# Expert part of a hybrid layer: the first slots' copies, a bank and row numbers in another order, and the second largest slot last, with the other second norms under its products

## Chip, cores and metric

The kernel runs on one core of one Trainium2 chip. The metric is the device time of one execution, in microseconds (us), as the median over runs.

## What is computed

One decoder layer over 1,024 rows of 1,024 numbers: attention over a sliding window beside a gated spatial mix, a first norm that gives h, then 32 experts of which each row uses four, and a second norm. Cut to the part that matters here:

```python
h = layer_norm(ALPHA * x + mix, ln1_g, ln1_b)
top_vals, top_idx = top_k(h @ w_router + b_router, 4)      # of 32 experts
gates = softmax(top_vals)
def expert(xb, e):                                         # rows xb of h sent to expert e
    gt = minimum(xb @ w_gate[e] + b_gate[e], 7.0)
    up = clip(xb @ w_up[e] + b_up[e], -7.0, 7.0)
    return (gt * sigmoid(1.702 * gt) * (up + 1.0)) @ w_down[e] + b_down[e]
y = layer_norm(ALPHA * h + sum of gates * expert rows, ln2_g, ln2_b)
```

## The kernel before, in words

The first 390 us or so hold projections, attention, first norm and router; the expert part fills the rest. The experts are sorted by their number of rows into 32 slots with fixed numbers of columns (`CAP`, 256 down to 88); a flag at the end tells whether one had too many, and `rescue` would then do its rows once more. `ORDER` says which slot is worked when: the largest and the smallest first, then pairs of a large and a small one, at the end the two of `LAST`.

A slot has three products: g and u (from the rows, to the hidden values) and d (back). Each is cut into two halves, so there are 192 pieces, in the order that `plan` writes out. A piece needs 2 MB of weights, loaded by SP's queue as two tiles into a ring of seven `raw` buffers (`loads`). ACT makes the upper half-precision part of each (`hi`, L962), DVE the rest (`lo`, L966), into one of three `wsp` buffers, two pieces ahead of PE. `multiply` (L1126) is 96 matmuls: four blocks of 128 outputs, eight steps, three products of parts. Its results lie in PSUM banks pg, pu or pd, two of each. ACT adds the bias to g (`gate1`, `gv`, L1158) and takes its gelu (`gate2`), DVE does u (`glu1`, `glu3`, `glu5`), the result is `hid`; DVE copies d to `yt` (`down`, L1199). PE turns `yt` (`turn`, L1209), ACT weights the rows (`combine`) and POOL scatters them, adding, into a tensor acc in memory, which started with ALPHA h.

A slot's rows are found and brought so: DVE writes a one-hot (`onehot`, L1081), PE multiplies it with the row numbers (`rows_of`, L1091), ACT writes indices and gates (`index`), POOL gathers (`gather`), PE transposes (`xpose`, L1112), ACT copies to `xt` (`xcopy`, L1117; in slot 0 DVE does one of each two). A list of events, `ev`, hangs these steps on the pieces; the tables in `SEQ` order the steps on one piece. All engines work strictly through their own rows in the order in which the program writes them. `rank` gives the places of the rows; its last part casts V on ACT and PP on DVE.

At the end the eight blocks of acc are loaded back (`loads`, L1006), two to a load, and normed: the `s` steps in `FIN` are sums on ACT and a power on POOL (`sums`, L1338 to L1342), the `a` steps two operations on DVE and a store (`first_norm`, L1351, L1352). Rows of the last slot aren't final in acc then: they are gathered apart to `xl`, get the slot's contribution (`last1`), sums (`last2`), their norm (`last3`, L1243, L1244) and are scattered over the output. DVE and PE write the flag (`flags`).

## Time and profile before

| | |
|---|---|
| median of 3 runs | 1703.27 us (1702.88 to 1704.67) |
| the profiled execution | 1707.27 us, span 1705.5 us |
| granted TensorE clock, mean | 0.974 of full speed |
| busy: PE, DVE, ACT, POOL | 1609.5 (94%), 1445.6 (85%), 1219.4 (72%), 310.2 us (18%) |
| DMA | 501.11 MB, mean 294 GB/s |

Times in the trace count from the start of the span. An engine is busy while it works on an instruction; waiting is not busy. A share is a mean over parts with different limits, so it tells which engine to look at and not what a change in one part is worth.

### The profile page before, as it was taken

To read this page: it belongs to the slowest core of one execution; us is meant where nothing else is said; L and a number is where in the kernel's file an instruction comes from. 1 tells how busy PE (TensorE), PEld (TensorE's weight loads), DVE (VectorE), ACT (ScalarE), POOL (GpSimd) and SP (SyncE) were. 2 spreads that over 40 slices of the span, in tenths; PEclk is the share of its full clock that TensorE was granted. 3 is DMA by queue.
4 is the path that set the end of the run, shared out by engine and by line. 5 is a ranking of instruction groups with operands and counts; after the bars stand their busy time and mean duration, and the time that the engine had idled before them with its cause. 6 is when DMAs were issued, how large, how long until landed. Compare 5 with 4: busy or idle time off the path is not lost.

```text
span 1705.5 us, 51018 instructions
## 1 busy us (share of the span) xinstructions
PE 1609.5 (94%) x21947; PEld 1509.6 (89%) x21947; DVE 1445.6 (85%) x2106; ACT 1219.4 (72%) x1662; POOL 310.2 (18%) x260
## 2 busy tenths in 40 slices
...
GB/s 270 91 122 38 164 99 100 87 322 197 226 348 338 329 324 337 343 343 343 339 355 338 364 343 373 364 361 371 358 364 352 377 339 382 361 382 359 366 348 139
DMA packets 86714, 501.11 MB, mean 294 GB/s; under 512 B 14210, under 2 KB 14226, under 8 KB 37330
## 3 DMA queue, kind: packets, MB, share of 16 engines
...
## 4 chain that ended last, share of the span: by engine, by line
PE 71%; ACT 3%; issue 1%; DVE 1%; DMA 1%; POOL 0%; POOLq 0%; DVEq 0%; ACTq 0%
PE pu L1126 22%; PE pg L1126 22%; PE pd L1126 21%; PE pt L1209 2%; PE pt L1112 2%; ACT wsp L962 1%; PE pt L1091 1%; DMA wsp<-htab,ix 1%; ACT xg L1338 0%; ACT gv L1158 0%; DMA raw<-w_d 0%; ACT xg L1340 0%; ACT y L1215 0%; DVE raw L1352 0%; ACT xt L1117 0%
## 5 line engine op out<-in xcount | busy, mean ns | idle before, releaser
L1126 PEld LDWEIGHTS <-wsp 128*128 128x128 f16 x18432 | 1152.7, 98 | 24.0 <-issue 9.6
L966 DVE SCALAR_TENSOR_TENSOR wsp<-raw,wsp 128x2048 f16<-128x2048 f32 x384 | 868.6, 2287 | 108.3 <-ACT wsp L962 102.4
L962 ACT ACTIVATE wsp<-raw 128x2048 f16<-128x2048 f32 x384 | 717.0, 1910 | 22.2 <-PE pu L1126 19.4
L1126 PE MATMUL pg<-xt,wsp 128*128 128x96 f16 (+30 forms) x6144 | 399.1, 226 | 4.2 <-ACT gv L1158 2.6
L1126 PE MATMUL pd<-hid,wsp 128*128 128x96 f16 (+30 forms) x6144 | 397.2, 226 | 4.2 <-ACT hid L1186 2.8
L1126 PE MATMUL pu<-xt,wsp 128*128 128x96 f16 (+30 forms) x6144 | 398.2, 226 | 0.0
L1217 POOL DMA_INDIRECT acc<-y,ix x49 | 99.7, 2034 | 820.7 <-ACT y L1215 534.2
L956 POOL DMA_INDIRECT xg<-htab,ix x49 | 78.7, 1607 | 257.4 <-ACT ixf L940 224.3
L1158 ACT ACTIVATE gv<-pg,bi 128x96 f32<-128x96 f32 (+30 forms) x256 | 78.7, 377 | 51.4 <-PE pg L1126 51.4
L1215 ACT ACTIVATE y<-pt,gw 128x512 f32<-128x512 f32 (+7 forms) x98 | 61.9, 685 | 41.9 <-PE pt L1209 41.9
L1117 ACT COPY xt<-pt 128x1024 f16<-128x1024 f16 (+29 forms) x98 | 70.8, 776 | 17.3 <-PE pt L1112 16.5
L1186 ACT ACTIVATE hid<-uv 128x384 f16<-128x384 f32 (+28 forms) x102 | 47.7, 499 | 43.6 <-DVE uv L1183 43.6
L179 DVE TENSOR_TENSOR wl<-rw,wh 128x512 fp32r<-128x512 f32 x56 | 38.8, 739 | 40.2 <-ACT wh L178 40.2
L198 PE MATMUL psp<-xh,wh 128*128 128x512 f32 x160 | 65.5, 409 | 6.8 <-ACT xh L189 6.8
L199 PE MATMUL psp<-xl,wh 128*128 128x512 f32 x160 | 65.2, 408 | 3.9 <-DVE xl L191 3.8
L948 ACT ACTIVATE ixf<-pt,dummy 128x1 f32<-128x1 f32 (+7 forms) x47 | 11.8, 251 | 75.9 <-PE pt L1091 75.9
L200 PE MATMUL psp<-xh,wl 128*128 128x512 f32 x160 | 64.5, 403 | 0.0
L1160 DVE SCALAR_TENSOR_TENSOR uv<-pu,bi 128x384 f32<-128x384 f32 (+28 forms) x102 | 53.7, 527 | 5.5 <-PE pu L1126 5.4
L527 PE MATMUL psp<-woh,mh 128*128 128x512 f32 x128 | 54.7, 428 | 3.5 <-issue 3.5
L1209 PE MATMUL pt<-iden,yt 128*128 128x128 f32 (+7 forms) x400 | 52.1, 273 | 2.6 <-ACT gv L1158 1.4
L1172 ACT ACTIVATE gv<-gv 128x384 f32<-128x384 f32 (+28 forms) x102 | 47.8, 512 | 8.2 <-DVE gv L1169 8.2
L529 PE MATMUL psp<-wol,mh 128*128 128x512 f32 x128 | 51.4, 402 | 1.1 <-DVE wol L489 1.1
...
## 6 DMA issues: line engine op xcount, KB each, us to landing
raw<-w_g SPq DMA_DIRECT2D x128, 1024.0 KB
raw<-w_u SPq DMA_DIRECT2D x128, 1024.0 KB
raw<-w_d SPq DMA_DIRECT2D x128, 1024.0 KB
...
```

The source lines that it names most:

```text
L198: nc.tensor.matmul(pt, wh[:, k], xh[h, k], start=(k == 0), stop=False)
L199: nc.tensor.matmul(pt, wh[:, k], xl[h, k], start=False, stop=False)
L200: nc.tensor.matmul(pt, wl[:, k], xh[h, k], start=False, stop=(k == 7))
L956: self.nc.gpsimd.indirect_dma_start(out=x[:m], out_offset=None, in_=self.htab, in_offset=bass.IndirectOffsetOnAxis(ap=self.IDX[j, o][:m], ...
L962: self.nc.scalar.activation(self.W[i][:, 0, 4 * z:4 * z + 4], self.RAW[i, z], AF.Copy, scale=WS)
L966: self.nc.vector.scalar_tensor_tensor(t[:, 1], self.RAW.pop((i, z)), WS, t[:, 0], op0=OP.mult, op1=OP.subtract, accum_out=self.FL[:, self. ...
L1117: (nc.vector.tensor_copy if j == 0 and z else nc.scalar.copy)(XT[j][:, z, :, o:o + m], XP.pop((j, o, z))[:, :, :m])
L1126: nc.tensor.matmul(out, w[:, wz, k, 128 * fc:128 * fc + 128], x[:, xz, k], start=(n == 0), stop=(n == 23))
L1158: nc.scalar.activation(out[:, q], src[:, q], AF.Identity, scale=1.0 / (HS * WS), bias=bi[:, c + q:c + q + 1])
L1209: nc.tensor.transpose(pt[:m, i], YT[j][:, 4 * g + i, o:o + m], self.iden)
L1215: nc.scalar.activation(y[:m, 512 * g:512 * g + 512], YP.pop((j, o, g))[:m].rearrange("p a b -> p (a b)"), AF.Copy, scale=GW[j, o][:m])
L1217: nc.gpsimd.indirect_dma_start(out=self.acc, out_offset=bass.IndirectOffsetOnAxis(ap=IDX[j, o][:m], axis=0), in_=y[:m], in_offset=None, co ...
```

## The change

Three things. **The first slots:** slot 1's transposes and copies go from ahead of the first product into its middle; the copy of slot 0's second 128 rows goes ahead of `rank`'s casts; g of slot 1 writes to a bank pd; the row numbers of slot 3 follow u of slot 0, and the indices of slots 2 and 3 come later in ACT's order; the gelu's table is loaded by a small extra activation. **The order of slots:** `LAST` ends with slot 244 columns wide instead of 124; the 124 goes into the pairs. **The end:** slot 30's d pieces come ahead of slot 31, whose six pieces stand last without a gap; `FIN` spreads the second norms over them; the last piece is cut into 128 and 116 columns, each turned, added and normed by itself with statistics from DVE. The scatter of the last slot's rows to acc is left to `rescue`. The diff, with pools, the rescue and removed functions cut:

```diff
@@ -29,8 +29,7 @@
 LA = 2
-FIN = {-3: ["s0", "s1"], -2: ["s2"], -1: ["s3", "a0", "a1"], 0: ["a2"],
-       1: ["c1", "s4", "s5", "a3", "s6", "a4", "c2", "s7", "a5", "a6", "a7", "c3"]}
+FIN = {-4: ["s0", "s1", "a0"], -3: ["s2", "s3"], -2: ["a1", "a2", "s4", "a3", "s5", "a4", "s6", "a5", "s7"]}
...
@@ -39,7 +38,7 @@
 ORD = ["q0", "q1", "k", "g0", "q2", "g1", "q3", "v", "u0", "u1", "u2", "u3"]
-LAST = [18, 19]
+LAST = [18, 1]
...
@@ -981,9 +980,9 @@
         s, e = NE - 2, NE - 1
-        seq += [("g", s, 0), ("d", s - 2, 0), ("u", s, 0), ("d", s - 2, 1), ("g", s, 1), ("d", s - 1, 0), ("u", s, 1),
-                ("d", s - 1, 1), ("g", e, 0), ("d", s, 0), ("d", s, 1), ("u", e, 0), ("g", e, 1), ("u", e, 1), None,
-                ("d", e, 0), ("d", e, 1)]
+        seq += [("g", s, 0), ("d", s - 2, 0), ("u", s, 0), ("d", s - 2, 1), ("g", s, 1), ("u", s, 1)]
+        seq += [("d", j, hf) for j in (s - 1, s) for hf in range(2)]
+        seq += [("g", e, 0), ("u", e, 0), ("g", e, 1), ("u", e, 1), ("d", e, 0), ("d", e, 1)]
...
@@ -1100,11 +1099,11 @@
 
-        XP = {}
+        XP, TL = {}, NE - 1
 
         def xpose(j, o, m):
             if o == 0:
-                XT[j] = pm.tile([128, 2, 8, CAP[j]], F16, name=f"xt{j % 2}", bufs=1)
+                XT[j] = pm.tile([128, 2, 8, CAP[j]], F16, name=f"xt{j % 2 if j < TL else 0}", bufs=1)
...
@@ -1139,11 +1138,18 @@
             for f, nf in groups(j):
-                pt = ps.tile([128, 512], F32, name="p" + kind, bufs=2)
+                pt = ps.tile([128, 512], F32, name="pd" if (kind, j, hf) == ("g", 1, 0) else "p" + kind, bufs=2)
                 pt = PG[kind, j, hf, f] = pt[:, :nf * n].rearrange("p (f n) -> p f n", n=n)
                 if (kind, j, hf) != ("d", NE - 1, 0):
                     for q in range(nf):
                         mm(pt[:, q], w, x, f + q)
+                if i == 0 and f == 0:
+                    for q, (o, m) in enumerate(subs(1)):
+                        xpose(1, o, m)
+                        xcopy(1, o, m)
+                if (kind, j, hf, f) == ("g", TL, 0, 0):
+                    turn(TL - 1, *subs(TL - 1)[0])
+                    combine(TL - 1, *subs(TL - 1)[0])
...
@@ -1210,40 +1216,71 @@
             m = whole(m)
-            y = pm.tile([128, D], F32, name="y", bufs=2)
+            y = pmm.tile([128, D], F32, name="y", bufs=2)
             for g in range(2):
                 nc.scalar.activation(y[:m, 512 * g:512 * g + 512], YP.pop((j, o, g))[:m].rearrange("p a b -> p (a b)"),
                                      AF.Copy, scale=GW[j, o][:m])
             nc.gpsimd.indirect_dma_start(out=self.acc, out_offset=bass.IndirectOffsetOnAxis(ap=IDX[j, o][:m], axis=0),
                                          in_=y[:m], in_offset=None, compute_op=OP.add)
 
-        TL = NE - 1
-
-        def last1(j):
-
-            m = whole(CAP[j])
-            y = self.yl = pm.tile([128, D], F32, name="y", bufs=2)
+        def last_turn(q, g):
+
+            o, m = subs(TL)[q]
+            pt = YP[q, g] = ps.tile([128, 4, 128], F32, name="pt", bufs=2)
+            for i in range(4):
+                nc.tensor.transpose(pt[:whole(m), i], YT[TL][:, 4 * g + i, o:o + whole(m)], self.iden)
+
+        def last_add(q, g):
+
+            cs = slice(512 * g, 512 * g + 512)
+            o, m = subs(TL)[q]
+            m = whole(m)
+            if g == 0:
+                self.yl.append((pmm.tile([128, D], F32, name="y", bufs=2), IDX[TL, o], m))
+            y, x = self.yl[q][0], self.xl[q]
+            nc.scalar.activation(y[:m, cs], YP.pop((q, g))[:m].rearrange("p a b -> p (a b)"), AF.Copy, scale=GW[TL, o][:m])
+            nc.vector.tensor_add(x[:m, cs], x[:m, cs], y[:m, cs])
+            nc.vector.bn_stats(self.lbn[:m, q, g], x[:m, cs])
+            if g:
+                self.scale1(self.lbn[:, q], self.lmv[:, q])
+
+        def last_norm(q):
+
+            x, mv, (y, ix, m) = self.xl[q], self.lmv[:, q], self.yl[q]
             for g in range(2):
                 cs = slice(512 * g, 512 * g + 512)
-                nc.scalar.activation(y[:m, cs], YP.pop((j, 0, g))[:m].rearrange("p a b -> p (a b)"),
-                                     AF.Copy, scale=GW[j, 0][:m])
-                nc.vector.tensor_add(self.xl[:m, cs], self.xl[:m, cs], y[:m, cs])
-
...
+                nc.vector.scalar_tensor_tensor(x[:m, cs], x[:m, cs], mv[:m, 0:1], self.l2g[:m, cs], op0=OP.subtract, op1=OP.mult)
                 nc.vector.scalar_tensor_tensor(x[:m, cs], x[:m, cs], mv[:m, 2:3], self.l2b[:m, cs], op0=OP.mult, op1=OP.add)
-            nc.gpsimd.indirect_dma_start(out=a["out"], out_offset=bass.IndirectOffsetOnAxis(ap=IDX[j, 0][:m], axis=0),
+            nc.gpsimd.indirect_dma_start(out=a["out"], out_offset=bass.IndirectOffsetOnAxis(ap=ix[:m], axis=0),
                                          in_=x[:m], in_offset=None)
+
+        def last_out(q, src):
+            o, m = subs(TL)[q]
+            nc.vector.scalar_tensor_tensor(YT[TL][:, 4:8, o:o + m], src, 1.0 / (ZS * WS), bc(BI[TL], 20, 4, m),
+                                           op0=OP.mult, op1=OP.add)
+
+        def last_piece():
+
+            w, pt = W.pop(n - 1), []
+            for q, (o, m) in enumerate(subs(TL)):
+                t = ps.tile([128, 512], F32, name="pg", bufs=2)
+                pt.append(t[:, :4 * m].rearrange("p (f n) -> p f n", n=m))
+                for f in range(4):
+                    mm(pt[q][:, f], w, HID[TL][:, :, :, o:o + m], f)
+                    if q and f == 1:
+                        last_turn(0, 1)
+                        last_add(0, 1)
+                if q == 0:
+                    for r in range(2):
+                        last_turn(r, 0)
+                    last_out(0, pt[0])
+                    for r in range(2):
+                        last_add(r, 0)
+            last_out(1, pt[1])
+            last_turn(1, 1)
+            last_norm(0)
+            last_add(1, 1)
+            last_norm(1)
...
@@ -1251,15 +1288,12 @@
             for k, (f, d) in enumerate(((onehot, 11), (rows_of, 10), (index, 9), (gather, 8)) if j > 1 else ()):
-                i = j - 2 + k // 2 if j < 4 else max(t - d, t0 + k)
-                ev.setdefault((i, f.__name__), []).append((f, (j,)))
+                i = (0, 0, 1, 1, 1, 2, 3, 3)[4 * j - 8 + k] if j < 4 else max(t - d, t0 + k)
+                ev.setdefault((i, "gather" if j < 4 and k == 2 else f.__name__), []).append((f, (j,)))
             for q, (o, m) in enumerate(subs(j)):
-                for f in (xpose, xcopy):
-                    ev.setdefault((max(t - 3 + q + (j == 2), q - 2 if j == 0 else 0), f.__name__), []).append((f, (j, o, m)))
-                if j == TL:
-                    ev.setdefault((at["d", j, 1] + 2, "turn"), []).append((turn, (j, o, m)))
-                    continue
-                for f in (turn, combine):
+                for f in (xpose, xcopy) if j != 1 else ():
+                    ev.setdefault((max(t - 3 + q + (j in (2, TL)), q - 2 if j == 0 else 0), f.__name__), []).append((f, (j, o, m)))
+                for f in (turn, combine) if j < TL - 1 else ():
...
@@ -1269,12 +1303,13 @@
         next(rank)
-        for i in range(-4, n + 4):
+        for i in range(-4, n):
             run(i, "index", "turn", "xpose")
             if i == -4:
                 next(rank)
             if i == -1:
                 lo(1, 0)
+                run(i, "xcopy")
...
@@ -1311,26 +1346,37 @@
                     run(i, st)
+            if i == n - 1:
+                self.flags1(pmm)
+                for b in (6, 7):
+                    self.first_norm("a", b)
+                last_piece()
+                break
+            if i == 0:
+                warm = pm.tile([128, 1], F32, name="warm")
+                nc.scalar.activation(warm, self.mhalf[:, 0:1], AF.Gelu_apprx_sigmoid)
             if 0 <= i < n and pieces[i][0]:
                 multiply(i)
             run(i, "rows_of")
             if i == n - 7:
                 self.norm_rows(*(x.bitcast(F32) for x in self.XT[:2]))
-                self.fmv = pmm.tile([128, 4, NB + 1], F32, name="fmv")
-                self.xl, self.junk = (x.bitcast(F32) for x in self.XT[2:])
-            if i == n - 5:
+                self.fmv = pmm.tile([128, 4, NB], F32, name="fmv")
+                self.lmv = pmm.tile([128, 2, 4], F32, name="lmv")
+                self.lbn = pmm.tile([128, 2, 2, 6], F32, name="lbn")
+                nc.vector.memset(self.lbn, 0.0)
+                self.xl, self.yl = [x.bitcast(F32) for x in self.XT[2:]], []
+                self.junk = pm.tile([128, D], F32, name="oh", bufs=1)
+            if i == n - 6:
                 self.summed = True
-                m = whole(CAP[TL])
-                nc.gpsimd.indirect_dma_start(out=self.xl[:m], out_offset=None, in_=self.acc,
-                                             in_offset=bass.IndirectOffsetOnAxis(ap=IDX[TL, 0][:m], axis=0))
+                for x, (o, m) in zip(self.xl, subs(TL)):
+                    m = whole(m)
+                    nc.gpsimd.indirect_dma_start(out=x[:m], out_offset=None, in_=self.acc,
+                                                 in_offset=bass.IndirectOffsetOnAxis(ap=IDX[TL, o][:m], axis=0))
             self.loads()
             for k in FIN.get(i - n, ()):
-                if k[0] == "c":
-                    (last1, last2, last3)[int(k[1]) - 1](TL)
-                else:
-                    self.first_norm(k[0], int(k[1]))
-        self.flags(pmm)
-        assert not ev
+                self.first_norm(k[0], int(k[1]))
+        self.flags2(pmm)
+        assert not ev, ev
...
@@ -1360,8 +1406,12 @@
         nc.vector.tensor_reduce(bs, bad, axis=AX.X, op=OP.max)
-        pt = self.psm.tile([128, 512], F32, name="pt", bufs=2)
-        nc.tensor.matmul(pt[:, 0:1], self.ones16, bs, start=True, stop=True)
+        self.bs = bs
+
+    def flags2(self, pm):
+        nc = self.nc
+        pt = self.psm.tile([128, 512], F32, name="pu", bufs=2)
+        nc.tensor.matmul(pt[:, 0:1], self.ones16, self.bs, start=True, stop=True)
```

The first place is ACT's order ahead of the first product and behind it: `raw` and `wsp` are the weights, `pt` is slot 0's and slot 1's transposed rows, `pd` `rank`'s places. Before:

```order
L962 ACTIVATE wsp_3274<-raw_3154 128x2048
L1117 COPY xt_3508<-pt 128x8x128
L1062 CAST V<-pd 128x4x32 x4
L1117 COPY xt_3508<-pt 128x8x128
L1117 COPY xt_3578<-pt 128x704 x2
L962 ACTIVATE wsp_3275<-raw_3271 128x2048
L962 ACTIVATE wsp_3275<-raw_3272 128x2048
L948 ACTIVATE ixf<-pt,dummy 128x1
```

and in the changed kernel:

```order
L961 ACTIVATE wsp_3274<-raw_3154 128x2048
L1116 COPY xt_3508<-pt 128x8x128 x2
L1061 CAST V<-pd 128x4x32 x4
L961 ACTIVATE wsp_3275<-raw_3271 128x2048
L961 ACTIVATE wsp_3275<-raw_3272 128x2048
L1357 ACT_TABLE_LOAD
L1357 ACTIVATE warm<-mhalf 128x1
L1116 COPY xt_3635<-pt 128x704 x2
L1164 ACTIVATE gv<-pg,bi 128x256 x4
```

The second copy of slot 0 (128x8x128) now stands ahead of the casts of V, and slot 1's two copies (128x704) behind both `hi` of the next piece and a row that loads a table.

The second place is DVE's order in the last slot (`xg_3276`, `xg_3277` hold the norm's scale and shift, `raw` a block of acc, `xg_3486`, `xg_3487` the last slot's rows). Before, around the last copies of `yt`, and from the last slot's norm on:

```order
L1199 SCALAR_TENSOR_TENSOR yt<-pd,bi 128x2x124 x2
L1351 SCALAR_TENSOR_TENSOR raw_3151<-raw_3151,fmv,xg_3276 128x1024
L1352 SCALAR_TENSOR_TENSOR raw_3151<-raw_3151,fmv,xg_3277 128x1024
L1230 TENSOR_TENSOR xg_3486<-xg_3486,y 128x512 x2
L1351 SCALAR_TENSOR_TENSOR raw_3151<-raw_3151,fmv,xg_3276 128x1024
...
L1243 SCALAR_TENSOR_TENSOR xg_3486<-xg_3486,fmv,xg_3276 128x512
L1244 SCALAR_TENSOR_TENSOR xg_3486<-xg_3486,fmv,xg_3277 128x512
L1243 SCALAR_TENSOR_TENSOR xg_3486<-xg_3486,fmv,xg_3276 128x512
L1244 SCALAR_TENSOR_TENSOR xg_3486<-xg_3486,fmv,xg_3277 128x512
L1359 TENSOR_SCALAR oh<-FL 128x384
L1360 TENSOR_SCALAR oh<-FH 128x8
```

In the changed kernel, from the copies of the first d piece on, and from the copy of the last 116 columns on:

```order
L1398 SCALAR_TENSOR_TENSOR raw_3152<-raw_3152,fmv,xg_3277 128x1024
L1205 SCALAR_TENSOR_TENSOR yt<-pd,bi 128x2x244 x2
L1405 TENSOR_SCALAR oh<-FL 128x384
...
L1398 SCALAR_TENSOR_TENSOR raw_3153<-raw_3153,fmv,xg_3277 128x1024
L1259 SCALAR_TENSOR_TENSOR yt<-pg,bi 128x4x128
L1242 TENSOR_TENSOR xg_3486<-xg_3486,y 128x512
L1243 BN_STATS lbn<-xg_3486 128x6
L1242 TENSOR_TENSOR xg_3487<-xg_3487,y 128x512
L1243 BN_STATS lbn<-xg_3487 128x6
```

```order
L1259 SCALAR_TENSOR_TENSOR yt<-pg,bi 128x4x116
L1252 SCALAR_TENSOR_TENSOR xg_3486<-xg_3486,lmv,xg_3276 128x512
L1253 SCALAR_TENSOR_TENSOR xg_3486<-xg_3486,lmv,xg_3277 128x512
...
L1242 TENSOR_TENSOR xg_3487<-xg_3487,y 128x512
L1243 BN_STATS lbn<-xg_3487 128x6
L1598 BN_AGGR lmv<-lbn 128x2
L1599 TENSOR_SCALAR lmv<-lmv 128x1
L1252 SCALAR_TENSOR_TENSOR xg_3487<-xg_3487,lmv,xg_3276 128x512
L1253 SCALAR_TENSOR_TENSOR xg_3487<-xg_3487,lmv,xg_3277 128x512
```

All the plain norms (L1397, L1398) now stand ahead of the last slot's final copies of `yt`, the flag rows too, and behind the last copy are the norms of the last slot's two parts alone.

## Rows read from the trace of the kernel before

**Rows 1.** Page: busy time of PE, and the chain that ended last, by line.

```profile
PE 1609.5 (94%) x21947; PEld 1509.6 (89%) x21947; DVE 1445.6 (85%) x2106; ACT 1219.4 (72%) x1662; POOL 310.2 (18%) x260
PE pu L1126 22%; PE pg L1126 22%; PE pd L1126 21%; PE pt L1209 2%; PE pt L1112 2%; ACT wsp L962 1%; PE pt L1091 1%; DMA wsp<-htab,ix 1%; ACT xg L1338 0%; ACT gv L1158 0%; DMA raw<-w_d 0%; ACT xg L1340 0%; ACT y L1215 0%; DVE raw L1352 0%; A
```

**Rows 2.** Busy us (rows) of PE, PEld, DVE, ACT, POOL; clock, DMA, GB/s; by stretch.

```profile
1500.00:1600.00 100.00, 98.57 (x1607) 98.12 (x1605) 95.06 (x114) 78.66 (x84) 12.40 (x9) 1.00 1.00 371
...
sum 1150.00, PE 1144.66 PEld 1133.95 DVE 1048.58 ACT 932.26 POOL 172.55; mean PE 95.39 PEld 94.50 DVE 87.38 ACT 77.69 POOL 14.38
```

**Rows 3.** Timeline of PE at the start: start, duration, instruction, wait before it.

```profile
390.64 0.74 PE L1112 MATMUL pt<-iden,xg 88*128 88x88 f16 x8 [1.76 <-ACT xt L1117]
392.22 0.75 PE L1112 MATMUL pt<-iden,xg 88*128 88x88 f16 x8 [0.83 <-ACT xt L1117]
392.80 12.73 PE L1126 MATMUL pg<-xt,wsp 128*128 128x256 f16 x96
...
408.61 3.92 PE L1126 MATMUL pg<-xt,wsp 128*128 128x88 f16 x96 [2.62 <-ACT gv L1158]
418.99 0.65 PE L1091 MATMUL pt<-V,oh 128*128 128x4 f16 x16 [6.46 <-DVE oh L1081]
419.57 16.76 PE L1126 MATMUL pu<-xt,wsp 128*128 128x256 f16 x192
...
436.93 3.33 PE L1126 MATMUL pg<-xt,wsp 128*128 128x256 f16 x29
```

**Rows 4.** Busy time at the start, columns as in rows 2.

```profile
396.00:397.00 1.00, 1.00 (x6) 0.71 (x5) 1.00 (x1) 1.00 (x1) 0.00 (x0) 0.50 0.00 0
397.00:398.00 1.00, 1.00 (x11) 0.88 (x9) 1.00 (x3) 0.35 (x1) 0.00 (x0) 0.95 0.00 0
424.00:425.00 1.00, 1.00 (x10) 0.81 (x8) 0.80 (x1) 1.00 (x3) 0.00 (x0) 0.79 0.41 156
```

**Rows 5.** Timeline of PE in the last slot.

```profile
1656.72 0.26 PE L1126 MATMUL pd<-hid,wsp 128*128 128x124 f16 x1 [2.82 <-ACT hid L1186]
...
1663.72 5.39 PE L1126 MATMUL pd<-hid,wsp 128*128 128x124 f16 x96 [1.19 <-DVE yt L1199]
```

**Rows 6.** Busy time in the last slot, columns as in rows 2.

```profile
1657.00:1660.00 3.00, 2.83 (x28) 2.83 (x28) 1.61 (x3) 3.00 (x2) 0.00 (x0) 0.50 1.03 419
```

**Rows 7.** Timeline of POOL at the end.

```profile
1643.28 1.91 POOL L1217 DMA_INDIRECT acc<-y,ix  x1 [13.17 <-ACT y L1215]
1651.28 1.80 POOL L1324 DMA_INDIRECT xg<-acc,ix  x1 [6.10 <-DMA acc<-y,ix]
...
1677.96 1.56 POOL L1342 TENSOR_TENSOR fmv<-fmv,mhalf 128x1 f32<-128x1 f32 x1
...
1684.42 0.55 POOL L1342 TENSOR_TENSOR fmv<-fmv,mhalf 128x1 f32<-128x1 f32 x1
...
1694.16 1.05 POOL L1245 DMA_INDIRECT out<-xg,ix  x1 [6.40 <-DVE flag L1372]
```

**Rows 8.** Timeline of DVE at the end.

```profile
1676.46 1.27 DVE L1351 SCALAR_TENSOR_TENSOR raw<-raw,fmv,xg 128x1024 f32<-128x1024 f32 x1
...
1679.03 1.28 DVE L1351 SCALAR_TENSOR_TENSOR raw<-raw,fmv,xg 128x1024 f32<-128x1024 f32 x1
...
1687.80 1.28 DVE L1352 SCALAR_TENSOR_TENSOR raw<-raw,fmv,xg 128x1024 f32<-128x1024 f32 x1 [0.81 <-POOL fmv L1342]
1689.00 0.74 DVE L1243 SCALAR_TENSOR_TENSOR xg<-xg,fmv,xg 128x512 f32<-128x512 f32 x1
```

**Rows 9.** Timeline of ACT at the start.

```profile
388.83 0.88 ACT L1062 CAST V<-pd 128x128 f16<-128x128 f32 x4 [4.05 <-DVE PP L1060]
389.56 1.03 ACT L1117 COPY xt<-pt 128x1024 f16<-128x1024 f16 x1
```

**Rows 10.** Timeline of PE: one product of a 244-column slot.

```profile
547.90 10.19 PE L1126 MATMUL pg<-xt,wsp 128*128 128x244 f16 x96
```

**Rows 11.** Waits of SP's queue, 437 to 1650: us in total, times, longest.

```profile
SPq L1018 <- DVE wsp L966: 869.8, 297, 8.6
```

More of the change, by code (lines that the diff above doesn't have):

```diff
@@ L838, in open_more @@
     def open_more(self):
-        p = self.pr2 = self.held.enter_context(self.tc.tile_pool(name="pr2", bufs=1, side="right"))
+        p = self.pr2 = self.held2.enter_context(self.tc.tile_pool(name="pr2", bufs=1, side="right"))
         self.RW += [p.tile([128, 4, 512], F32, name=f"raw{i}") for i in range(4, 7)]
@@ L1176, in glu1 @@
             if c == 0:
-                HID[j] = pm.tile([128, 2, 8, n], F16, name=f"hid{j % 2}", bufs=2)
+                HID[j] = pm.tile([128, 2, 8, n], F16, name=f"hid{j % 2 if j < TL else 0}", bufs=2)
             uv = UV[j, c] = tmp("uv", n, nf)
@@ L1226, in last1 @@
+        def last_norm(q):
+            x, mv, (y, ix, m) = self.xl[q], self.lmv[:, q], self.yl[q]
             for g in range(2):
                 cs = slice(512 * g, 512 * g + 512)
-                nc.scalar.activation(y[:m, cs], YP.pop((j, 0, g))[:m].rearrange("p a b -> p (a b)"),
-                                     AF.Copy, scale=GW[j, 0][:m])
-                nc.vector.tensor_add(self.xl[:m, cs], self.xl[:m, cs], y[:m, cs])
-        def last2(j):
-            m = whole(CAP[j])
-            self.sums(self.xl[:m], self.fmv[:m, :, NB], self.junk[:m])
-            nc.gpsimd.indirect_dma_start(out=self.acc, out_offset=bass.IndirectOffsetOnAxis(ap=IDX[j, 0][:m], axis=0),
-                                         in_=self.yl[:m], in_offset=None, compute_op=OP.add)
@@ L1353, in first_norm, with flags1 @@
             nc.sync.dma_start(a["out"][128 * b:128 * b + 128], x)
-    def flags(self, pm):
+    def flags1(self, pm):
         nc = self.nc
```

14 lines of the change are left out of this document (6 added, 8 removed).

## The prediction

> **What bounds the kernel now.** I read the page's shares first, then the busy time by stretch, then the two ends of the expert part row by row. TensorE (PE) is busy 94% of the span, and the chain that ended last runs through its three products g, u and d, about a fifth of the span each [rows 1]. In the middle of the expert part nothing else is the limit: from 500 to 1650 us PE is idle 1150.0 − 1144.7 = 5.3 us in all, although in the stretch 1500 to 1600 VectorE (DVE) is busy 95.06 and the DMA engines are at a share of 1.00 [rows 2]. So a gain must come from the two ends, where PE waits. At the start the reader sees PE wait 1.76 and 0.83 us for copies of slot 1's transposes, 2.62 us for a PSUM bank of g (released by ScalarE's, ACT's, copy of gv), and 6.46 us for DVE's one-hot of slot 3 [rows 3]. The granted clock is 0.50 (1.2 of 2.4 GHz) until 397 us, and 0.50 again after the long wait, until about 424.4 (0.79 over that microsecond) [rows 4]. At the other end PE waits 2.82 and 1.19 us within the last slot [rows 5], runs at 0.50 behind the first of these [rows 6], and its last product ends at 1663.72 + 5.39 = 1669.1 us. The scatter that finishes the output is issued at 1694.16 [rows 7]: 25.1 us in which PE does almost nothing and DVE and ACT work off second norms [rows 8]. From that issue to the span's end (1705.5) pass 11.3 us.
>
> **The change part by part.** All terms are against the profiled execution: 1707.27 us, a span of 1705.5 and 1.8 around it. It lies 4.0 us above the median, 1703.27, to which I apply the same difference.
>
> *1. The start: −12.8 us.* Before, g of slot 0 starts at 392.80, after slot 1's transposes. Now it needs only slot 0's copy, which ACT ends at 389.56 + 1.03 = 390.59 behind the four casts of V [rows 9]; put ahead of these, it ends 0.88 to 1.9 earlier, so I start the product at 389.5. The two transposes (0.74 + 0.75, both in [rows 3]) now stand within the product: −3.3 + 1.5 = −1.8. The bank wait goes, since g of slot 1 takes a free bank of d: −2.6. The 6.46 wait goes, as slot 3's row numbers follow u of slot 0: −6.5. What hides it is that product (96 × 256 columns, about 10.5 us by the 244-column row [rows 10]); the one-hot, which ended near 418.9 behind two DVE `lo`, ends near 412.5 when these come forward with ACT's `hi`, and the product near 418. Were the cover gone the one-hot would cost what it lacks, up to 6. Behind the vanished wait the clock need not fall: from 419.57 to 424.4 half the work was lost, 4.85/2 = −2.4. That makes −13.3; I give back 0.5 for a PSUM bank of u that slot 1's product must get from DVE. The half clock at the head of g I let cost what it did; if it lasts until 397 as before, although g starts 3.3 earlier, the term is 1.6 smaller. With g of slot 0's second half now near 424.1 (before 436.93), bounds: −13.5 to −10.
>
> *2. The middle: +2.5 us.* The 32 slots have the same columns in sum, so PE's products cost the same. But the pairs lose 244 − 124 = 120 columns, which come back in the last slot alone: (10.19 − 3.92)/(244 − 88) = 0.0402 us per column and product [rows 3, 10], × 120 × 6 = 28.9 us of PE time. DVE, ACT and the queues must do the pairs' unchanged work (24 halves of weights a pair) in that much less time. By the two tables of slots the fifteen pairs ahead of the last had 290 columns on average and get 282, the last five of them 280 and 273; a pair's d products run beside the next pair's g and u, and over such a mix the lightest stretch goes from 277 to 270. DVE's work per pair stays, so its share, 95.06% at 1500 us, becomes 95.06 × 277/270 = 97.5% [rows 2]: still under PE, with less slack for one late row. At 95% PE lost 1.4 us in 100, elsewhere 0.4 (3.9 in the other 1,050). I let the last 420 us lose 0.6 per 100 more, 2.5 in all. Bounds 0, since the slack may do, and +8, if the whole 420 us lose 2 more per 100.
>
> *3. The last slot's products: +4.2 us.* Before, they hold 2.82 + 1.19 = 4.0 of waiting [rows 5] and 3 us at half clock [rows 6], 1.5 lost. Now count from the start of the last slot's first product: four of 244 columns at 10.0 each and slot 30's turn (0.9) end at 40.9. The d product waits about 1.5 for `hid`, whose last steps stand on DVE, and ends at 52.4, its last half's first 128 columns at 57.8. Meanwhile DVE, free at about 45.4, has five norms ahead of slot 31's `yt`: two rows each, 2.57 us from one norm to the next [rows 8], 12.9 in all, then two copies: PE's turn waits until 59.7 (1.9 us). It turns 8 (0.9) and does two of four 116-column blocks (2.45), to 63.05. The next turn needs `yt` of the first half, which stands on DVE behind the flag rows (1.1), two more norms (5.2) and its own 0.6: 66.6, a wait of 3.5. With 0.4 and 2.45 the last product ends at 69.5. Waits 1.5 + 1.9 + 3.5, turns 0.9 + 0.4 that were behind the products before, and 0.3 for splitting 244 into 128 and 116: 8.5. The clock fell during the 2.82 wait, so it can during the 3.5 one; the last 2.45 us would then double. I put in half of that, 1.2. Slot 30's scatter moves into the first of these products: POOL issues it near 7, from such an issue to what waits for it passed 8.0 us before (1643.28 to POOL's gather at 1651.28) [rows 7], SP's four loads of acc and POOL's two gathers follow from 15 on, and ACT's first sum comes near 26; I find about 5 us of room, and cost it at nothing. Sum 8.5 + 1.2 − 4.0 − 1.5 = +4.2; bounds 0 (the norms do not hold DVE up) and +9 (both waits and the half clock at full).
>
> *4. From the last product to the last scatter: −15.3 us.* Behind the last product now stand, for its second half: the copy of `yt` (0.65), the first half's norm (four operations of 128×512, 0.74 each [rows 8], 2.95), then the add and its statistics (0.65 each, taken as nearly such an operation), their two small rows (0.35), POOL's power (0.2 + 0.55), and four more norm operations (2.95), with about 0.8 of hand-overs: 9.75 instead of 25.05. The eight norms that stood there are under the products, which is why term 3 is positive. The scatter before waited for the plain rows of the output too; now the last of these is issued near 66 on the same count, 13 us ahead of the scatter at 79.3, where the whole way from the last plain norm's end (1687.80 + 1.28) to the scatter took 5.1 [rows 7, 8]. Bounds −17 to −12.
>
> On POOL's power one rule speaks against the change. The row shows 1.56 us while DVE's norm runs beside it and 0.55 when it has ended [rows 7]; so each power under the products can be 1.0 late. I leave the sum as it is, because s3 to s7 are ready more than 2 us before DVE's backlog comes to them, and at the two halves of the last slot DVE has nothing to run meanwhile. The Trainium skill (SBUF — State Buffer, "SBUF: two separate sides") says that DVE and GpSimd share one port pair as an exclusive lock, against a DVE operation with two SBUF inputs for its whole length; the trace's 1.56 against 0.55 agrees. If this lock held the last two powers back as well, the sum would be 2.0 us worse, by the same rows.
>
> *5. After the scatter: 0.* Its 11.3 us hold the same operation and the same end of program.
>
> Sum: −12.8 + 2.5 + 4.2 − 15.3 = −21.4: the profiled execution near 1685.9, the median near 1681.9.
>
> **The rivals.** *(a) The pairs are paced by DVE or ACT after all.* Speaking for it: DVE 95.06 at 1500 us. Against: at 95.06 PE still lost only 1.4 us in 100, and 97.5 is under 100. Price: term 2 at +8 or somewhat over, 1687 to 1693.
> *(b) The pairs are paced by the loads: slower.* The place is SP's load queue from about 1100 us on; the price is the 28.9 us of PE time that then reappear at the end without the pairs getting shorter. For it: a DMA share of 1.00 at 371 GB/s [rows 2]. If 371 is the most that this mix of transfers can have, no pair can shrink: −21.4 − 2.5 + 28.9 = +5.0, 1708. It decides once it takes back some 24 of the 28.9 (the 21.4 and the 2.5 that the sum already holds), that is if the loads allow less than a fifth of the 2.8% by which pairs get lighter. Against: the queue waited 870 us for buffers that DVE must free [rows 11], so loads were issued late, not served late.
> *(c) The start is not kept.* Slot 0's second half comes 12.8 us earlier, but its weights are made by the same ACT and DVE rows; if these come only 5 to 8 us earlier, 1686 to 1690. Against: DVE and ACT waited there for PE.
> *(d) The last slot runs late.* The loads of acc wait for slot 30's scatter; the sums stand in ACT's order ahead of copies of gv, so a late load stops PE. Beyond the 5 us of room each us counts: 1685 to 1690.
> *(e) More is gained:* the last slot's waits of 6.9 us and the half clock do not appear, 1673 to 1675.
>
> **How the numbers follow.** My forecast has 0.58 (own range 1676 to 1687), (a) 0.12, (b) 0.09, of which 0.06 slower, (c) 0.09, (d) 0.07, (e) 0.05. I leave out (b) and half of (e), which is 0.115, and take 1674 to 1692. About 0.2% (3.4 us) is what a measurement of this kernel tells from no change; faster means under 1699.9. That is all but (b) and the far ends of (a) and (c): 0.88 faster, 0.05 the same, 0.07 slower.
>
> **What would show it.** Right: g of slot 0 starts near 389.5, no wait over 1 us before slot 0's second half near 424, clock at full by 397 and not down again; PE idle under 10 us from there to the last slot; a PE wait of 2 to 4 us ahead of the last 48 matmuls with DVE named as releaser; 9 to 11 us between the last product and the last scatter. Wrong: waits of PE on `lo` or of ACT on loads spread over the pairs (a, b), a gap at the third to fifth product (c), or ACT waiting for a load of acc in the last slot (d).

## The result, and the profile after

The changed kernel takes 1680.68 us (median of 4 runs, 1679.05 to 1681.70); the kernel before, on the same chip, 1703.97. The ratio is 0.986 (95% interval 0.9843 to 0.9877). The profiled execution took 1681.08, span 1679.3, 26.2 less than that of before; PE is now busy 96% of it. The page's busy times, and its chain by engine:

```profile
PE 1608.3 (96%) x22043; PEld 1510.3 (90%) x22043; DVE 1452.2 (86%) x2109; ACT 1217.3 (72%) x1654; POOL 317.5 (19%) x260
...
PE 79%; DVE 8%; ACT 3%; issue 3%; DMA 1%; POOL 0%; DVEq 0%; ACTq 0%; POOLq 0%
```

The chain of before has 1% of DVE, but the two shares can't be compared: those of before make 77%, since that chain can be followed back to 377 us only, and of the 8% now the larger part lies ahead of 390 us. What the change brought is the end of the chain: from 1633.9 us to the last scatter it runs through DVE's rows almost alone, some 31 us of 36. PE at the start (the answer to [rows 3]; line numbers are 1 lower):

```profile
386.74 1.89 PE L1111 MATMUL pt<-iden,wsp 128*128 128x128 f16 x16 [0.87 <-DMA wsp<-htab,ix]
...
390.37 7.61 PE L1125 MATMUL pg<-xt,wsp 128*128 128x256 f16 x48 [0.20 <-issue]
397.82 0.79 PE L1111 MATMUL pt<-iden,xg 88*128 88x88 f16 x16
398.44 5.41 PE L1125 MATMUL pg<-xt,wsp 128*128 128x256 f16 x48
...
404.24 3.93 PE L1125 MATMUL pd<-xt,wsp 128*128 128x88 f16 x96
408.01 10.65 PE L1125 MATMUL pu<-xt,wsp 128*128 128x256 f16 x96
...
419.04 3.93 PE L1125 MATMUL pu<-xt,wsp 128*128 128x88 f16 x96
...
423.58 10.64 PE L1125 MATMUL pg<-xt,wsp 128*128 128x256 f16 x96
```

No wait of 1.8, 2.6 or 6.5 us is left, and g of slot 0's second half starts at 423.58 (436.93 before). Counted from the second transposes of slot 0, which began at 386.00 before and begin at 386.74 now, that is 36.8 instead of 50.9 us: −14.1. Busy time by stretch, columns as in [rows 2]:

```profile
394.00:395.00 1.00, 1.00 (x7) 0.73 (x6) 1.00 (x1) 0.98 (x2) 0.00 (x0) 0.53 0.45 123
395.00:396.00 1.00, 1.00 (x12) 0.90 (x10) 1.00 (x3) 0.99 (x2) 0.00 (x0) 1.00 0.99 418
404.00:420.00 16.00, 16.00 (x243) 14.83 (x242) 12.70 (x15) 14.53 (x23) 2.74 (x2) 1.00 0.63 214
500.00:1500.00 1000.00, 998.24 (x16413) 994.17 (x16411) 933.64 (x1144) 835.94 (x1011) 159.32 (x102) 1.00 0.99 363
1400.00:1500.00 100.00, 100.00 (x1663) 99.79 (x1661) 95.16 (x116) 84.99 (x96) 14.37 (x9) 1.00 1.01 377
1533.00:1538.00 5.00, 5.00 (x37) 4.94 (x36) 3.75 (x4) 5.00 (x8) 2.72 (x3) 0.50 0.90 301
1648.00:1656.00 8.00, 3.76 (x56) 3.34 (x56) 7.75 (x12) 1.27 (x2) 0.00 (x0) 1.00 0.34 134
```

The clock rises at 395 and does not fall again in the start. From 500 to 1500 us PE is idle 1000 − 998.2 = 1.8 us, with DVE at 93.4 in 100. In the same view of before it is idle 3.0:

```profile
500.00:1500.00 1000.00, 997.01 (x15913) 987.11 (x15911) 911.41 (x1124) 813.80 (x990) 150.88 (x100) 1.00 0.98 353
```

One place alone lost much time, where slot 31's rows are found. DVE's row and PE there:

```profile
1527.86 2.28 DVE L1080 TENSOR_TENSOR oh<-iota,PP 128x2048 f16<-128x2048 f16 x1
...
1530.19 0.55 PE L1090 MATMUL pt<-V,oh 128*128 128x4 f16 x16 [2.54 <-DVE oh L1080]
...
1532.71 1.10 PE L1215 MATMUL pt<-iden,yt 128*112 128x128 f32 x4 [1.47 <-ACT gw L941]
1533.61 9.29 PE L1125 MATMUL pd<-hid,wsp 128*128 128x164 f16 x96
```

A wait of 2.5 us for DVE's one-hot, one of 1.5 for ACT's gates, and behind them half clock from 1533 to 1538: these 96 matmuls of 164 columns take 9.3 us, where 7.0 is usual: 6.3 us in all. In the last slot PE has the waits that follow (compare [rows 5]):

```profile
1634.59 7.58 PE L1125 MATMUL pd<-hid,wsp 128*128 128x244 f16 x71 [0.44 <-DVE hid L1196]
...
1648.68 1.45 PE L1231 MATMUL pt<-iden,yt 128*128 128x128 f32 x8 [1.16 <-DVE yt L1205]
...
1656.06 0.63 PE L1231 MATMUL pt<-iden,yt 128*128 128x128 f32 x4 [3.49 <-DVE yt L1259]
1656.53 2.60 PE L1125 MATMUL pg<-hid,wsp 128*128 128x116 f16 x48
1661.01 0.63 PE L1231 MATMUL pt<-iden,yt 128*128 128x128 f32 x4 [1.88 <-DVE yt L1259]
```

The last product ends at 1656.53 + 2.60 = 1659.1. DVE over the same time, then POOL (compare [rows 7, 8]):

```profile
1635.03 1.28 DVE L1397 SCALAR_TENSOR_TENSOR raw<-raw,fmv,xg 128x1024 f32<-128x1024 f32 x1
...
1655.23 0.68 DVE L1259 SCALAR_TENSOR_TENSOR yt<-pg,bi 128x512 f32<-128x512 f32 x1
...
1660.23 0.63 DVE L1259 SCALAR_TENSOR_TENSOR yt<-pg,bi 128x464 f32<-128x464 f32 x1
...
1665.52 0.74 DVE L1252 SCALAR_TENSOR_TENSOR xg<-xg,lmv,xg 128x512 f32<-128x512 f32 x1
1666.72 0.75 DVE L1253 SCALAR_TENSOR_TENSOR xg<-xg,lmv,xg 128x512 f32<-128x512 f32 x1 [0.46 <-POOL lmv L1600]
...
1668.17 0.75 DVE L1253 SCALAR_TENSOR_TENSOR xg<-xg,lmv,xg 128x512 f32<-128x512 f32 x1
```

```profile
1645.60 1.47 POOL L1388 TENSOR_TENSOR fmv<-fmv,mhalf 128x1 f32<-128x1 f32 x1
...
1660.39 0.55 POOL L1600 TENSOR_TENSOR lmv<-lmv,mhalf 128x1 f32<-128x1 f32 x1 [13.20 <-DVE lmv L1599]
...
1665.68 1.00 POOL L1600 TENSOR_TENSOR lmv<-lmv,mhalf 128x1 f32<-128x1 f32 x1 [0.29 <-DVE lmv L1599]
1669.21 1.03 POOL L1254 DMA_INDIRECT out<-xg,ix  x1 [2.53 <-DVE over L1419]
```

From the last product to the last scatter pass 1669.2 − 1659.1 = 10.1 us, before 25.1; from that scatter to the span's end 10.1, before 11.3.

### The profile page after: what moved, and what is told of

It is laid out like the page before. It is cut to its first block, busy times and chain, and to the rows that moved or that the text cites. A ratio compares the mean times of both kernels' runs of the same rounds, so it can differ in the third digit from the quotient of the medians.

```text
span 1679.3 us, 51203 instructions
## 1 busy us (share of the span) xinstructions
PE 1608.3 (96%) x22043; PEld 1510.3 (90%) x22043; DVE 1452.2 (86%) x2109; ACT 1217.3 (72%) x1654; POOL 317.5 (19%) x260
## 3 DMA queue, kind: packets, MB, share of 16 engines
q0 software_dynamic: 12848, 44.86, 10.1%
## 4 chain that ended last, share of the span: by engine, by line
PE 79%; DVE 8%; ACT 3%; issue 3%; DMA 1%; POOL 0%; DVEq 0%; ACTq 0%; POOLq 0%
PE pu L1125 22%; PE pg L1125 22%; PE pd L1125 21%; PE pt L1215 2%; PE pt L1111 2%; PE psp L526 1%; PE psp L528 1%; PE psc L373 1%; PE psp L527 1%; ACT wsp L961 1%; DVE s L406 1%; PE psp L197 1%; PE pt L1090 1%; PE psp L198 1%; PE psp L199 1%
## 5 line engine op out<-in xcount | busy, mean ns | idle before, releaser
L1125 PE MATMUL pg<-xt,wsp 128*128 128x96 f16 (+30 forms) x6048 | 394.5, 226 | 0.2 <-issue 0.2
L1125 PE MATMUL pd<-hid,wsp 128*128 128x96 f16 (+30 forms) x6048 | 388.0, 226 | 0.4 <-DVE hid L1196 0.4
```

What stands on the lines that cost most here:

```text
L1125: nc.tensor.matmul(out, w[:, wz, k, 128 * fc:128 * fc + 128], x[:, xz, k], start=(n == 0), stop=(n == 23))
```

## Experiments

Each edit is against the changed kernel unless said. As the spans of single executions differ already ahead of slot 0's transposes (they began between 383.4 and 387.5), the last three columns count from the start of the second of these in each profiled execution: to slot 0's second half, to the last scatter, to the span's end.

| kernel | median us | ratio to before (95%) | second half | scatter | end |
|---|---|---|---|---|---|
| before | 1703.97 | | 50.9 | 1308.2 | 1319.5 |
| changed | 1680.68 | 0.986 (0.9843–0.9877) | 36.8 | 1282.5 | 1292.6 |
| e1_start_only | 1691.06 | 0.991 (0.9897–0.9924) | 37.0 | 1293.8 | 1304.4 |
| e2_end_only | 1693.35 | 0.9924 (0.991–0.9937) | 51.1 | 1297.5 | 1307.4 |
| e3_rows3_first | 1688.29 | 0.9893 (0.9877–0.9908) | 44.3 | 1290.4 | 1300.3 |
| e7_bank_pg | 1681.63 | 0.985 (0.9836–0.9863) | 37.8 | 1283.9 | 1293.8 |
| e13_index_first | 1683.53 | 0.9877 (0.9859–0.9895) | 40.9 | 1287.2 | 1297.3 |
| e4_rows31_later | 1677.87 | 0.9842 (0.9829–0.9856) | 36.5 | 1279.9 | 1289.9 |
| e10_onehot31_early | 1676.52 | 0.9828 (0.9815–0.9841) | 36.3 | 1278.9 | 1288.8 |
| e5_copy_first | 1680.18 | 0.985 (0.9837–0.9864) | 36.7 | 1282.5 | 1292.8 |
| e6_copies_act | 1677.98 | 0.9839 (0.9825–0.9852) | 36.6 | 1280.2 | 1290.2 |
| e12_a1_early | 1679.65 | 0.9845 (0.9832–0.9859) | 36.5 | 1280.1 | 1290.1 |
| e8_last164 | 1691.47 | 0.9922 (0.9908–0.9935) | 37.1 | 1294.6 | 1304.6 |
| e11_all | 1671.95 | 0.98 (0.9787–0.9814) | 36.5 | 1273.8 | 1284.0 |

The medians of before, run beside each group of these kernels, lay between 1704.7 and 1706.3, so kernels of different groups are compared by their ratios. With intervals of about ±0.14%, 2.3 us, these don't tell e4, e5, e6, e7, e12 and e13 from the changed kernel; what is said of those rests on the traces. There the last three columns are one execution each, and differ by 0.1 to 0.6 us already in the start, which the edits at the end don't touch. From the last slot's first product to the last scatter, however, the way is 78.9 us in the changed kernel, in e5 and in e7.

**The start alone, and the end alone.** e1 is the kernel before with the hunks on `xpose`, `xcopy`, the bank, the events of slots 1 to 3 and the small activation; e2 is the changed kernel without them.

> The kernel before with the changes to the first slots alone (copies, bank, row numbers, table); slots, plan and end as before. If the two ends act apart from each other, as the sum in the prediction has it, it gains the start alone: 12 to 14 us under the kernel before, near 1691, and its trace has g of slot 0's second half near 423.5 and the last slot's waits unchanged (2.8 and 1.2). Rival: the gain is given back in the pairs, because DVE, ACT and the loads there get their work no earlier; then 3 to 10 us and PE's idle time between 500 and 1650 rises from 5 to over 8.

> The changed kernel with the first slots as before; slots, plan and end as changed. If the parts act apart, it stands 9 to 13 us under the kernel before, near 1693, with the start's waits of 2.6 and 6.5 back, and the two differences (this one and the one with the start alone) add up to the whole of 23 within 2 us. Rival: the end's gain needs the earlier start, or the waits at slot 31's one-hot come from it; then the sum misses the whole by over 4 us and those waits (2.5 and 1.5 near 1530) are gone here.

By the last column they gain 15.1 and 12.1, together 27.2 of the whole's 26.9; by the ratios 0.9 and 0.76% against 1.4%, the sum 0.26% above the whole, about what the intervals allow. By medians the sum within 2 us that was expected did not come: 15.1 and 12.8 make 28.0, against 23.3, or against 24.6 of e7, which ran beside them and does not differ from the changed kernel. The traces speak for parts that act apart: e1's last slot has its waits as before (2.89 and 0.91 us), e2's start takes 51.1 us as before, and e2 has the wait of 2.5 us for slot 31's one-hot too, so that does not come from the earlier start. Where the 3 to 5 us of the medians come from stays open.

**The start's parts.**

```diff
-                i = (0, 0, 1, 1, 1, 2, 3, 3)[4 * j - 8 + k] if j < 4 else max(t - d, t0 + k)
+                i = (0, 0, 1, 1, 1, 1, 3, 3)[4 * j - 8 + k] if j < 4 else max(t - d, t0 + k)
```

> The changed kernel, but the row numbers of slot 3 are again multiplied ahead of u of slot 0. DVE's one-hot ends near 413 there and PE comes to it near 408. If the order on PE is what removed the wait, PE waits 4.9 us there and the clock falls for part of the 4 us behind: 5 to 7.5 us slower than the changed kernel. Rival: ACT's new order (indices behind gelu and hi) made the one-hot early enough by itself; then under 2 us.

Measured: 7.4 us longer to slot 0's second half. The wait is 4.85, and the two u products behind it (192 matmuls, 256 and 88 columns) take 16.94 us, where they took 10.65 + 3.93 without it:

```profile
413.23 0.65 PE L1090 MATMUL pt<-V,oh 128*128 128x4 f16 x16 [4.85 <-DVE oh L1080]
413.81 16.94 PE L1125 MATMUL pu<-xt,wsp 128*128 128x256 f16 x192
```

So the order on PE removed the wait, and the half clock behind it (granted 0.50 from 413 to 419 us) cost 2.4 more.

```diff
-                pt = ps.tile([128, 512], F32, name="pd" if (kind, j, hf) == ("g", 1, 0) else "p" + kind, bufs=2)
+                pt = ps.tile([128, 512], F32, name="p" + kind, bufs=2)
```

> The changed kernel, but g of slot 1 takes a bank pg again. The prediction gave the bank 2.6 us: then PE waits about 2.6 us for ACT's copy of gv ahead of that product and the time rises by that. Rival, which I now hold likelier: with the indices of slot 2 out of the way, ACT copies the first half of gv at 399.6 to 400.5, well ahead of 404.2 when PE wants the bank; then no wait and a difference under 0.5 us, and the bank's change did nothing.

No wait ahead of that product in PE's timeline (no bracket behind the row), and no difference that the ratios show; of the 0.95 us in the table 0.6 is a longer wait of PE for `rank`'s copies ahead of g of slot 0 (1.10 instead of 0.50) and 0.4 that product's first half at half clock (8.01 instead of 7.61):

```profile
405.92 3.93 PE L1125 MATMUL pg<-xt,wsp 128*128 128x88 f16 x96
```

```diff
-                ev.setdefault((i, "gather" if j < 4 and k == 2 else f.__name__), []).append((f, (j,)))
+                ev.setdefault((i, "gather" if j == 3 and k == 2 else f.__name__), []).append((f, (j,)))
```

> The changed kernel, but ACT writes slot 2's indices ahead of gv of slot 0 again, as the kernel before did; the bank of g of slot 1 stays pd. With the run that has the new order and a bank pg, this fills the table of the two: if bank and order each remove the wait of 2.6 us by itself, PE does not wait here either, and from slot 0's second transposes to slot 0's second half pass 36.5 to 38 us, as in the changed kernel (36.8; before 50.9). Rival: ACT's order is needed for more than the bank, because gv, gelu, hi and DVE's one-hot of slot 3 come 1.7 us later; then PE waits for one of them and it is 39 or more.

The rival held: 4.1 us longer. With the bank pd the wait of 2.6 stays away, but `hi` now begins 3.0 us later (20.9 instead of 17.9 from the transposes), and DVE's copy of u, in its order behind `lo`, frees a PSUM bank too late. PE in front of u of slot 1:

```profile
419.27 5.51 PE L1125 MATMUL pu<-xt,wsp 128*128 128x88 f16 x96 [2.31 <-DVE uv L1166]
```

2.31 us of wait and 1.6 for the half clock behind it (5.51 instead of 3.93). ACT's order is worth about 4 us; the bank nothing once the order is new. The rest of the start's 14.1 us has no run of its own: the earlier first product (3.6 instead of 6.8 us behind the second transposes, with 0.6 for slot 1's transposes inside it), and the gelu's table, whose row of 1.28 us on ACT stood at 411.08 before and stands at 394.60 now.

**Slot 31's one-hot.**

```diff
-                i = (0, 0, 1, 1, 1, 2, 3, 3)[4 * j - 8 + k] if j < 4 else max(t - d, t0 + k)
+                i = (0, 0, 1, 1, 1, 2, 3, 3)[4 * j - 8 + k] if j < 4 else max(t - d, t0 + k) + (j == TL and k > 0)
```

> The changed kernel, but PE multiplies the one-hot of slot 31 one piece later (its indices and gather too). In the changed kernel PE waits there 2.5 us for DVE's one-hot, then 1.5 us for ACT's gates, and the next 96 matmuls of 164 columns take 9.3 instead of 7.0 us at a lower clock. If this is the order of one wide slot and not a lack of DVE time, the 6.3 us go: 1674 to 1676. Rival: DVE is late there because the light pairs leave it no slack; the wait then shows up one piece on, or ahead of products waiting for lo, and under 2 us are gained.

Neither: 2.7 us of 6.3. DVE's 2.3 us of one-hot still stand at the same place in its order, and PE now waits for the row behind it, the copy of yt, with a lower clock after:

```profile
1529.77 0.65 PE L1215 MATMUL pt<-iden,yt 128*112 128x128 f32 x4 [2.63 <-DVE yt L1205]
1530.26 8.63 PE L1125 MATMUL pd<-hid,wsp 128*128 128x164 f16 x96
```

e10 puts all four steps four pieces earlier (`- 4 * (j == TL)` in place of the last term).

> The changed kernel, but all four steps that find slot 31's rows (DVE's one-hot, PE's multiplication, ACT's indices, POOL's gather) hang on pieces four earlier, ahead of the last pair's small products, where DVE has more slack. If the cost was a one-hot of 2.3 us in DVE's row at a place without slack, the waits of 2.5 and 1.5 us, the half clock behind them and the wait for yt that the run with PE's multiplication alone later showed all go: 5 to 6.5 us under the changed kernel, 1674 to 1676. Rival: DVE simply has no time left in the light pairs, wherever the one-hot stands; then PE waits for lo instead and it gains no more than the 2.7 of that run.

The waits of 2.5 and 2.6 are gone; one for ACT's gates is left:

```profile
1507.28 0.60 PE L1111 MATMUL pt<-iden,xg 126*128 126x126 f16 x8 [1.50 <-ACT gw L941]
```

The last slot starts 5.2 us earlier (1198.4 instead of 1203.6 from the transposes, 0.6 of it already in the start), but the scatter only 3.6. The rest went to the clock in the last slot: behind the same wait of 3.5 us as in the changed kernel, the last 48 matmuls take 4.85 us instead of 2.60, at a granted clock of 0.50 (third row, columns as in [rows 2]), and DVE waits 1.51 for them:

```profile
1648.11 1.09 PE L1231 MATMUL pt<-iden,yt 128*128 128x128 f32 x4 [3.50 <-DVE yt L1259]
1648.99 4.85 PE L1125 MATMUL pg<-hid,wsp 128*128 128x116 f16 x48
...
1650.00:1652.00 2.00, 2.00 (x24) 2.00 (x23) 1.93 (x4) 0.00 (x0) 0.00 (x0) 0.50 0.00 0
...
1653.88 0.64 DVE L1259 SCALAR_TENSOR_TENSOR yt<-pg,bi 128x464 f32<-128x464 f32 x1 [1.51 <-PE pg L1125]
```

**What sets the end.** In e5 `last_piece` runs `last_out(0, ...)` ahead of the norms of blocks 6 and 7. In e6 `down` and `last_out` copy the last slot's yt on ACT, a row for each block of 128 outputs:

```diff
+            for f in range(4):
+                nc.scalar.activation(YT[TL][:, 4 + f, o:o + m], src[:, f], AF.Identity, scale=1.0 / (ZS * WS), bias=BI[TL][:, 20 + f:21 + f])
```

In e12 "a1" moves from step −2 to step −4 of `FIN`.

> The changed kernel, but DVE copies yt of the last piece's first 128 columns ahead of the last two plain norms. PE's wait of 3.5 us ahead of the last 48 matmuls falls below 1. If PE's products still set the end, the time falls by 2.5 to 3.5 us. Rival: in the last slot DVE sets the end (it is busy almost without a break from 1635 to 1669), so the same rows in another order end at the same time: within 0.7 us of the changed kernel, although PE's wait is gone.

> The changed kernel, but the last slot's yt is copied from PSUM by ACT (16 rows with the bias of one block each) and not by DVE (four rows, 2.5 us in sum); ACT is nearly idle from 1645 on. If DVE sets the end of the last slot, the time falls by what leaves its chain, 2 to 2.5 us, less about 0.4 where ACT's copy is longer on the way. Rival: PE's products or their turns set it; then the waits of 1.2 and 3.5 us on yt go too and 3.5 to 5 us are gained. Third: hand-overs eat it, under 1 us.

> The changed kernel, but the second plain norm (2.6 us on DVE) follows the first at once, near 1621, where DVE idles 1.4 us a little later, instead of standing behind the last hid. If DVE's row sets the end from there on, the end comes 2.6 us earlier, and PE's wait of 1.2 us for yt falls away while the one of 3.5 stays near it. Rival: it delays lo of the last piece and gv by up to 1.2 us and hid with them; then under 1 us is gained.

In e5 PE's last product ends 3.6 us earlier and the scatter at the same time, 1282.5:

```profile
1651.75 2.60 PE L1125 MATMUL pg<-hid,wsp 128*128 128x116 f16 x48
1659.90 1.09 PE L1231 MATMUL pt<-iden,yt 128*128 128x128 f32 x4 [5.55 <-DVE yt L1259]
```

The wait went behind the product, to the last turn. In e6 PE has almost no wait and its products end 5.6 us earlier, but the scatter comes 2.2 earlier, about what left DVE's row (2.5 us); DVE has work from its second norm to the last without a pause longer than 0.47:

```profile
1648.97 2.60 PE L1125 MATMUL pg<-hid,wsp 128*128 128x116 f16 x48
1652.02 1.07 PE L1236 MATMUL pt<-iden,yt 128*128 128x128 f32 x4 [0.45 <-ACT yt L1265]
```

```profile
1662.57 0.75 DVE L1258 SCALAR_TENSOR_TENSOR xg<-xg,lmv,xg 128x512 f32<-128x512 f32 x1 [0.47 <-POOL lmv L1605]
```

e12 gains 2.4 of its 2.6. Counted from the last slot's first product, the scatter comes after 76.9 us in e6 and in e12, 2.0 sooner than in the changed kernel and in e5; in e12 DVE waits 0.47 for the last product, which is partly at half clock there. So DVE's row sets the end, as long as the clock does not fall behind PE's last wait: where it does, the way is 79.5 (e2, e3, e4: 4.22 us for the last 48 matmuls) or 80.5 (e10). The split of the last piece, the flag rows' earlier place and the statistics on DVE were not taken back one by one.

**The size of the last slot.** e8 has `LAST = [18, 8]`, 164 columns, and takes the statistics over the rows in use.

> The changed kernel with another slot last: 164 columns wide instead of 244 (split 128 and 36), the 244 back in the pairs. If the large last slot pays because its products cover the second norms, whose sums on ACT take 21.5 us and can start only when acc is loaded some 20 us into the slot, then its 60 us of products shrink to 40, the norms come out from under them, and of the 19 us of products that leave the slot most is lost again in the pairs: 5 to 10 us slower than the changed kernel. Rival: the size does not matter, the order of the end alone made the gain: within 2 us. Third: lighter pairs were the cost, then it is faster, by losing slot 31's late one-hot: 3 to 6 us.

12.0 us longer. The last slot starts 18.5 us later, and takes only 6.4 less to its scatter. ACT's first sum waits 3.5 us for the load of acc, and the sums stand ahead of `hid` in its order, so PE waits 8.1 us for hid; then ACT and PE:

```profile
1627.95 1.06 ACT L1384 ACTIVATE oh<-raw 128x1024 f32<-128x1024 f32 x1 [3.47 <-DMA raw<-acc]
...
1638.66 1.06 ACT L1384 ACTIVATE oh<-raw 128x1024 f32<-128x1024 f32 x1
...
1643.91 0.82 ACT L1192 ACTIVATE hid<-uv 128x328 f16<-128x328 f32 x2
```

```profile
1644.43 0.29 PE L1125 MATMUL pd<-hid,wsp 128*128 128x164 f16 x1 [8.14 <-ACT hid L1192]
...
1665.93 1.09 PE L1231 MATMUL pt<-iden,yt 128*128 128x128 f32 x4 [4.74 <-DVE yt L1259]
```

**All together.** e11 joins e10, e6 and e12, and puts `last_add(1, 1)` ahead of `last_norm(0)`.

> The three edits together: slot 31's rows found four pieces earlier, yt of the last slot copied by ACT, the second plain norm earlier, and besides the last part's add and statistics ahead of the first part's norm, so that POOL's two powers (0.45 us of waiting each) lie under DVE's row. If each acts on a row of its own on the chain, the gains add up: 6 + 2.4 + 2.6 + 0.9 = 11.9 us under the changed kernel, near 1669. Rival: once DVE is shorter, PE's products or the loads of acc set the end, and it stops 3 us or more above that, 1672 or more.

1671.95 us, ratio 0.98, 8.6 us off the changed kernel by the last column. That is the rival's time, but not for its cause: PE waits for nothing ahead of the last 48 matmuls (2.60 us), and DVE has no wait there. The single gains (3.7, 2.4 and 2.5) make 8.6 as well, which is a coincidence. e10 and e12 by themselves hold DVE's waits of 1.51 and 0.47 for a slowed last product, which are gone here, and the fourth edit took away DVE's waits of about 0.45 for POOL (one in the changed kernel, two in e6). Against these stands the last scatter: it now waits for the first one's landing, which the order before had kept out of the way. POOL:

```profile
1655.44 1.32 POOL L1259 DMA_INDIRECT out<-xg,ix  x1 [2.18 <-DVE xg L1258]
1659.98 0.98 POOL L1259 DMA_INDIRECT out<-xg,ix  x1 [3.21 <-DMA out<-xg,ix]
```

DVE's last norm ended at 1657.37 + 0.75 = 1658.1 there, 1.9 us ahead of the scatter; in the changed kernel these lie 0.3 apart. Whether e11 is faster without the fourth edit was not tried.

## Why the prediction was right

It said 1681.9, with the median at 1680.7. By its steps, against the profiled execution:

| step | predicted | measured | from |
|---|---|---|---|
| 1 start | −12.8 | −14.1 | 50.9 to 36.8 |
| 2 middle | +2.5 | +1.8 | what is left between the second half and the last product, +3.4, without step 3 |
| 3 last slot | +4.2 | +1.6 | waits 0.4 + 1.2 + 3.5, turns 1.3 + 0.5, split 0.2; before 4.0 + 1.5 |
| 4 to the scatter | −15.3 | −15.0 | 25.1 to 10.1 |
| 5 after it | 0 | −1.2 | 11.3 to 10.1 |

These make −26.9, what the last column of the table shows. The forecast of the median came closer than its terms, −21.4, by luck: the profiled execution of before, against which they were counted, lay 3.3 us above its median (1703.97) and that of after 0.4.

*Step 1* was right in mechanism for the row numbers and the clock (e3), and wrong for the bank: e7 and e13 show that ACT's order did it, and that without this order the wait goes to u of slot 1. It was 1.3 too small: both transposes inside the product took 0.6 us at one stretch, not 0.74 + 0.75, and the half us for u's bank was not needed: DVE's copy of u ends at 418.9, just ahead of 419.04, when PE writes there.

*Step 2* had nearly the right sum by another way, which is luck. The loss spread over the pairs did not come: idle time fell from 3.0 to 1.8 us between 500 and 1500, and up to the last slot, without the one place, from 5.3 to 2.1. What was lost, 6.3 us, was lost at that place, which the step did not look at: a one-hot of 256 columns in DVE's order among the small pieces, and the half clock behind it. Together that makes +3.1; the last 1.3 us to +1.8 are not traced.

*Step 3* named the wait of 3.5 us exactly and its cause; the wait for hid was 0.4 and not 1.5, that for yt 1.2 and not 1.9, and the clock did not fall in this execution, which is luck too (behind the same wait it fell in e2, e3, e4, e10 and e13, and not in e7). In the order of costs it missed that the wait of 3.5 costs nothing (e5): DVE sets the end, and PE's late product waits with it.

*Step 4* was right within 0.3, though DVE is still busy for 1.1 of the 10.1 us when the last product ends; where that product ended late, in e3, e4 and e10, 9.0 pass. It said that DVE has nothing to run while POOL takes the power; but the norm's first operation needs only the mean and runs then, so the last power took 1.00 us instead of 0.55 and DVE waited 0.46 behind it. This 1.00 us, and the 1.47 us of the powers beside the plain norms, agree with the lock that the Trainium skill (SBUF — State Buffer, "SBUF: two separate sides") describes. That it holds DVE in turn no row shows: the norms beside the powers keep their 1.28 us.

*Step 5* put nothing behind the scatter and 1.2 us less came; no run was made on that, and the cause is open.

*The rivals.* (b) fell: from 1400 to 1500 us PE is busy 100.00 with the loads at 377 GB/s, above the 371 that it took for a limit. (a) fell but for the one place. (c) and (d) did not come; (d)'s mechanism is what e8 shows. (e) did not come either: 5.1 of its 6.9 us of waits are there.
